# Two chained transformer blocks on one core: experts in pairs, attention by scaling and transposes, log decays in blocks of 16, no identity products

## The chip, the core and the metric

The kernel runs on one core of a Trainium2 chip (trn2), as one launch. The metric is the device time of that core in microseconds (us). TensorE (PE) multiplies, VectorE (DVE), ScalarE (ACT) and GpSimd (POOL) work on the elements, SyncE (SP) issues most of the transfers. [...]

## What is computed

Everything is fp32: 256 tokens of 1024 channels through a first block (twice: sparse attention A, latent attention B, a convolved FFN) and a second block. Cut to what the change touches:

```python
# first block, per layer: two attentions of 8 heads, 2 blocks of 128 queries
p = jax.nn.softmax(logits, axis=-1)                      # per head and block
y = jnp.einsum('bhts,bshd->bthd', p, v)
# second block, gated delta rule: on the context, then on the latent, both directions, chunks of 64
g = -jnp.exp(a_log) * jax.nn.softplus(a + dt_bias)
gc = jnp.cumsum(g.reshape(..., n, CHUNK), axis=-1)       # log decays, 4 chunks of 64
decay = jnp.where(incl, jnp.exp(gc[..., :, None] - gc[..., None, :]), 0.0)
# ... triangular solve per chunk, then a scan over the chunks; beside it RWKV-7:
s = s * w_t[..., None, :] + sa[..., :, None] * b_t[..., None, :] + v_t[..., :, None] * k_t[..., None, :]
# 32 experts in 4 groups, top-1 group and top-2 experts in it
hid = jax.nn.silu(einsum('td,edf->tef', t, w_gate[grp])) * einsum('td,edf->tef', t, w_up[grp])
out = out + jnp.einsum('tef,efd->td', hid * combine[:, grp, :, None], w_down[grp])
```

## The kernel before

Activations lie with channels on the partitions, [128, 8, 256]. Weights come in pieces of 512 KB (SyncE, `wload`), are split into a rounded high half (ScalarE, L452) and the rest (VectorE, L454), and each product is three (L460 to L462, `mm3`). PSUM banks come from `mm` (L421) in turn. The order of the instructions on each engine is set by the framework's scheduler from its own timeline, not by the order of the source, unless a block says otherwise.

By the span of the profile: attention of layer one to about 250 us, FFN and the context's delta rule to 600, attention of layer two 650 to 870, FFN and the context's RWKV to 1220, the latent's projections and delta rule to 1434, its RWKV (preparation to about 1540, then the steps over the chunks) to 1625, outputs to 1680, router, experts 1696 to 1962, last norm.

*Attention* (`attend`, L863). For 4 pairs of heads and 2 query blocks the logits go through the softmax: `pr` is the exponential (L886), `rs` the reciprocal of its row sum (L889). GpSimd multiplies the identity by each column of `rs` (`dg`, L892), TensorE multiplies `pr` by that diagonal (L896), which transposes and scales at once, with one bank per head; VectorE (block 0, L899) or ScalarE (block 1, L901) copies to `pt`, which is multiplied by `v` (L906).

*Log decays* (`gdn_core`, L1182; called once for the context, once for the latent). After softplus (lines to L1246) the prefix sums of 4 chunks are made token by token by 63 dependent adds of 64x4 (L1248); `zb`, `ez` and `tot` are made of them.

*Identity products* (L424). `mm` issues one product of the identity with itself into each new bank whose caller passes one of the names in `HEAT`: in the latent's triangular solves, in the RWKV's preparation, steps and outputs. Nothing reads them. `HEAT` is set in the streams of the latent's part only.

*Experts* (`moe`, L1776). Each expert has 64 slots. `gather` takes the rows of four experts' slots by one-hot products (L1861, L1873, L1880). In each of 16 steps two experts share the array's columns: `up` (L1903), then `down`: silu (L1910 to L1914), two transposes (L1917), copy to `mhT` (L1919), products (L1925), split; `scatter` (L1935) adds to four banks of sums. The weights come in 192 pieces of 512 KB, six for an expert, in two rings of 12 (`AHEAD`, L21) that take turns (`piece`, L2022, L2027); the first ring's are fetched before the experts begin. The source puts step i's `up` ahead of step i-1's `down` and scatter (`finish`), and the scheduler orders the rest.

Of the kernel before, what the change touches and what calls it, by code (L numbers as in the profile page):

```python
# [8 lines left out]
F32 = mybir.dt.float32  # L9
# [45 lines left out]
def col(v):  # L55
    """[..., n*128] -> [128, prod] channel-major columns."""
# [26 lines left out]
def t5_buckets():  # L83
    """bucket of rel = key - query, as t5_bucket has it, for rel in -255..255 (integers only)."""
# [48 lines left out]
def first_layer(i, l):  # L133
    """vectors, weight pieces and the small w_idx weights of one layer of the first block."""
# [48 lines left out]
def bias_tiles(rel_bias):  # L183
    """[128, 8*128 | 8*256]: bias of (query, head, key) for the two blocks of queries."""
# [14 lines left out]
def second_pieces(i):  # L199
# [15 lines left out]
    dn = np.asarray(i["moe_w_down_2"][0], F).reshape(32, 256, D)  # L215
    ps["moe"] = []
    for e in range(32):
        ps["moe"] += pieces(np.concatenate([g[e], u[e]], 1)) + pieces_wide(dn[e])
# [3 lines left out]
SECOND = ("in", "ada", "oa", "ob", "out", "moe")  # L222
# [44 lines left out]
def consts2(c):  # L267
# [4 lines left out]
    for d, tri in enumerate((up, lo)):  # L272
        # row j, column i: j before i (or with it) in the order of the direction, inside a chunk of 64
# [24 lines left out]
def layout(i):  # L298
    """the inputs as the program reads them, and where the parts lie"""
# [14 lines left out]
    for k in SECOND:  # L314
# [4 lines left out]
              "LORA": lora(i), "ROUTER": router(i)}  # L319
    return {k: np.ascontiguousarray(a) for k, a in arrays.items()}, c.at, v.at, woff, w2off  # L320


class Stream:
    """pool of data, scratch and PSUM banks of one strand of the work"""
# [6 lines left out]
class Tagged:  # L331
    """a pool whose tiles take the place of others by name"""
# [16 lines left out]
class Builder:  # L349
    def __init__(self, ctx, tc, I, at_c, at_v):  # L350
# [16 lines left out]
        # the other constants come between the first weights  # L367
# [11 lines left out]
    def phase(self, name, banks=0, t2=0, side="left", pb=1):  # L379
        """a pool that lives as long as a part of the work; with banks and t2 it has PSUM banks and scratch of its own"""  # L380
# [28 lines left out]
    def columns(self, name):  # L409
        """split columns of a layer's input, in place of the last ones"""  # L410
# [16 lines left out]
    def t2(self, name, dt=F32):  # L427
        """scratch of [128, 512]"""
# [6 lines left out]
    def wload(self, src, n=2):  # L435
        """split halves [128, 512] of a piece"""
# [13 lines left out]
    def split(self, hi, lo, x, scale=1.0):  # L450
        """hi + lo = scale * x, hi rounded to what one pass of the tensor engine carries"""
# [32 lines left out]
    def chunk_tok(self, srcs, kt, x, evac):  # L484
        """out[tokens, 512 cols]; evac(b, psum) per 128 tokens."""
# [12 lines left out]
    def rsqrt(self, y, a, t=None):  # L498
        """y = a ** -0.5 for positive a: an integer estimate, a step of third order and one of second"""
# [13 lines left out]
    def rsq(self, ps, rows, inv_n, eps=EPS):  # L513
        """(sums * inv_n + eps) ** -0.5 of sums [rows, 256 tokens] in PSUM, as [128, 2, rows] by token"""
# [11 lines left out]
    def to_rows(self, y, r0, n):  # L526
        """[128, 2, n] by token -> [n, 256]"""
# [7 lines left out]
    def rstd(self, x, kt, r):  # L535
        """r [128, 256] = rstd of the columns of x [128, kt, 256], on every partition"""
# [12 lines left out]
    def rstd_by_token(self, x, kt, cold=False):  # L549
        """[128, 2]: rstd of the columns of x [128, kt, 256], tokens on partitions; cold spares the tensor engine products"""  # L550
# [22 lines left out]
    def scaled(self, x, kt, gain, out):  # L573
        """split of x * gain"""
# [5 lines left out]
    def norm(self, x, kt, gain, out, shift=None, r=None):  # L580
        """rms norm over channels of x [128, kt, 256]: x * rstd * gain (+ shift), split."""
# [13 lines left out]
class First(Builder):  # L595
    """first block"""
# [4 lines left out]
    def mix(self, x, l, filler=None, ahead=None, after=None):  # L601
# [26 lines left out]
        # w_idx, tokens on partitions  # L628
# [39 lines left out]
        class Sums:  # L668
            """sums of squares of 8 query and 8 key heads, a few channels at a time"""
# [11 lines left out]
            def rstd(me, n, scale, name):  # L681
                """rstd * scale of 8 query heads [128, 2, 8] by token; rows() is rstd of 8 key heads [8, 256]"""
# [29 lines left out]
        # keys: rotated shared part  # L712
# [32 lines left out]
        # ---- branch A: rstd of queries and keys by token and head, keys normalized  # L745
# [32 lines left out]
        # ---- gates and merge  # L778
# [27 lines left out]
    def merge_a(self, gate, ya, wa):  # L806
        """gate = (1 + gate) * (ya @ wa)"""
# [6 lines left out]
    def merge_b(self, ga, gate, yb, mg, wb, together=False):  # L814
        """mg = split of (ga + (1 + gate) * (yb @ wb)) / 2"""
# [38 lines left out]
            # 0 for chosen keys, -1e30 for others, added to the bias of each head  # L854
# [8 lines left out]
    def attend(self, rq, v, logits, sels, yh, yl):  # L863
        """normalized, transposed probabilities and their products with v: y^T split, [128, 4, 256]"""
        V, S, G, T = self.V, self.S, self.G, self.T
        for t in range(4):
            # keys on partitions: [keys 0..127 x 256 queries | keys 128..255 x queries 128..255] per head
            pt = self.tmp([128, 2, 384], "pt", bufs=1)
            for b in range(2):
# [20 lines left out]
                dg = self.tmp([128, 2, 128], "dg", bufs=1)  # L890
                for p in range(2):
                    G.tensor_scalar(dg[:, p, :], self.ident, rs[:, p:p + 1], None, op0=ALU.mult)  # L892
                for p in range(2):
                    pp = self.mm()
                    for kk in range(b + 1):
                        T.matmul(pp[:, 128 * kk:128 * kk + 128], pr[:, p, 128 * kk:128 * kk + 128], dg[:, p, :],  # L896
                                 start=True, stop=True)
# [14 lines left out]
    def ffn(self, x, l, filler=None, r=None):  # L912
        """stops once before its first products; without r the norm comes after those"""
# [67 lines left out]
PIT = 4160  # pitch of the triangles of 64 in DRAM: the blocks of 16 on their diagonals lie 1040 apart  # L981
# [3 lines left out]
class Second(First):  # L985
    """second block"""
# [1232 lines left out]
```

## Time and profile before

| | |
|---|---|
| median of 3 runs | 1979.51 us (1979.09 to 1981.39) |
| span of the profiled execution, which is its own time here | 1980.6 us |
| mean granted clock of TensorE | 0.967 |
| busy: TensorE, its weight loads, VectorE, ScalarE, GpSimd | 94%, 79%, 63%, 44%, 17% |
| transfers | 341 MB, mean 172 GB/s |

The span is from the first to the last instruction. A matmul's row shows when its columns enter until its result is out; matmuls overlap, so the pace is read from the starts, not from the lengths. A group's idle time is what its engine stood before it, with what released it.

### The profile page before, as it was taken

How to read it: one execution, taken by the hardware profiler on the slowest of the kernel's cores; microseconds unless marked ns; L12 is line 12 of the kernel's file. 1: busy time of each engine (PE TensorE's matmuls, PEld its weight loads, DVE VectorE, ACT ScalarE, POOL GpSimd, SP SyncE). 2: the span in 40 equal slices, each digit the busy share in tenths (PEclk: the TensorE clock that was granted, in tenths of full speed). 3: DMA queues.
4: the chain of work that ended last, by engine and by line, in shares of the span. 5: the costliest groups of instructions: out<-in, count | busy, mean ns of one | idle time of the engine just before them, and what ended most of it. 6: DMA issues, size and time to landing. Idle time of an engine off the chain costs nothing. (4 is left out here: it accounts for less than half of the span.)

```text
span 1980.6 us, 38175 instructions
## 1 busy us (share of the span) xinstructions
PE 1860.3 (94%) x14934; PEld 1562.4 (79%) x14934; DVE 1242.6 (63%) x2742; ACT 879.5 (44%) x1728; POOL 337.2 (17%) x595
## 2 busy tenths in 40 slices
PE   8999999899999999999999998998998898999996
PEld 7868899698899878898898998888787788545453
DVE  7675578788676785568677766985474376322223
ACT  5555556565445555454445545564232133211111
POOL 0013101315010001205406300034126100000000
PEclk9999999899999999998999999999998899999998
DMA  7454355767645544363533553538003265799981
GB/s 251 143 181 156 111 160 170 270 204 230 183 124 184 154 155 139 88 209 110 145 118 99 150 166 123 160 119 206 27 12 44 37 235 201 298 385 364 390 331 65
DMA packets 169368, 341.43 MB, mean 172 GB/s; under 512 B 89400, under 2 KB 90048, under 8 KB 168288
## 3 DMA queue, kind: packets, MB, share of 16 engines
q1 hardware_dynamic: 160784, 308.75, 48.5%
q0 software_dynamic: 8400, 30.21, 4.1%
q8 instruction: 118, 1.93, 0.4%
q14 instruction: 66, 0.54, 0.1%
HBM read 325.87 MB, written 13.03 MB: 171 GB/s over the span
## 5 line engine op out<-in xcount | busy, mean ns | idle before, releaser
L454 DVE TENSOR_TENSOR wlo<-raw,whi 128x512 fp32r<-128x512 f32 x676 | 476.0, 714 | 234.5 <-ACT whi L452 212.5
L452 ACT ACTIVATE whi<-raw 128x512 fp32r<-128x512 f32 x676 | 421.3, 630 | 437.5 <-PE mm L461 272.7
L460 PE MATMUL mm<-hf,whi 128*128 128x256 f32 x672 | 192.5, 292 | 4.3 <-ACT whi L452 4.3
L461 PE MATMUL mm<-hf,whi 128*128 128x256 f32 x672 | 191.6, 289 | 2.5 <-DVE hf L454 2.5
L462 PE MATMUL mm<-hf,wlo 128*128 128x256 f32 x672 | 185.9, 292 | 4.9 <-DVE wlo L454 4.8
L460 PEld LDWEIGHTS mm<-hf,whi 128*128 128x128 f32 x672 | 129.7, 193 | 11.0 <-ACT whi L452 4.9
L461 PEld LDWEIGHTS mm<-hf,whi 128*128 128x128 f32 x672 | 129.5, 193 | 5.8 <-DVE hf L454 3.7
L462 PEld LDWEIGHTS mm<-hf,wlo 128*128 128x128 f32 x672 | 125.6, 193 | 9.5 <-DVE wlo L454 7.0
L460 PE MATMUL mm<-h,whi 128*128 128x256 f32 x448 | 130.7, 294 | 0.0
L461 PE MATMUL mm<-h,whi 128*128 128x256 f32 x448 | 128.9, 289 | 0.0
L462 PE MATMUL mm<-h,wlo 128*128 128x256 f32 x448 | 128.7, 291 | 0.0
L1903 PE MATMUL mm<-wm,xg 128*64 128x512 f32 x512 | 124.4, 597 | 0.0
L460 PE MATMUL mm<-hl,whi 128*128 128x256 f32 x384 | 111.1, 293 | 9.3 <-ACT hl L452 6.6
L462 PE MATMUL mm<-hl,wlo 128*128 128x256 f32 x384 | 109.7, 294 | 6.0 <-DVE wlo L454 5.8
L461 PE MATMUL mm<-hl,whi 128*128 128x256 f32 x384 | 111.7, 293 | 0.0
L461 PE MATMUL acc<-fl,whi 128*128 128x256 f32 x352 | 99.2, 286 | 0.0
L460 PE MATMUL acc<-fh,whi 128*128 128x256 f32 x352 | 98.7, 286 | 0.0
L462 PE MATMUL acc<-fh,wlo 128*128 128x256 f32 x352 | 96.2, 285 | 0.0
L1903 PEld LDWEIGHTS mm<-wm,xg 128*64 128x64 f32 x512 | 36.9, 137 | 66.6 <-issue 60.8
L460 PEld LDWEIGHTS mm<-h,whi 128*128 128x128 f32 x448 | 85.0, 190 | 4.6 <-issue 3.5
L461 PEld LDWEIGHTS mm<-h,whi 128*128 128x128 f32 x448 | 85.2, 190 | 3.7 <-issue 3.6
L892 POOL TENSOR_SCALAR dg<-cblob,rs 128x128 f32<-128x128 f32 x64 | 44.7, 708 | 253.3 <-DVE rs L889 213.3
(696 smaller groups left out, 4717.9 us busy)
## 6 DMA issues: line engine op xcount, KB each, us to landing
raw<-in_W_dram SPq DMA_DIRECT2D x336, 512.0 KB, 3.7
wm<-in_W_dram SPq DMA_DIRECT2D x192, 512.0 KB, 8.1
wada<-in_W_dram POOLq DMA_DIRECT2D x48, 512.0 KB, 6.5
lora<-in_LORA_dram SPq DMA_DIRECT2D x2, 1280.0 KB, 6.8
bm<-in_BIAS_dram SPq DMA_DIRECT2D x2, 1024.0 KB, 4.9
tri_ef<-tge SPq DMA_DIRECT2D x4, 512.0 KB, 8.2
gates<-gate SPq DMA_DIRECT2D x8, 256.0 KB, 4.5
mgate<-gates SPq DMA_DIRECT2D x2, 1024.0 KB, 5.1
```

The costliest lines, as they stand in the source:

```text
L452: self.S.activation(hi, x, AF.Copy, scale=scale)
L454: self.V.tensor_tensor(lo, x, hi, op=ALU.subtract)
L460: self.T.matmul(out, wh, xh, start=first, stop=False, **k)
L461: self.T.matmul(out, wh, xl, start=False, stop=False, **k)
L462: self.T.matmul(out, wl, xh, start=False, stop=last, **k)
L892: G.tensor_scalar(dg[:, p, :], self.ident, rs[:, p:p + 1], None, op0=ALU.mult)
L1903: T.matmul(gu[64 * p:64 * p + 64, :], xe[:, k, 128 * j + 64 * p:128 * j + 64 * p + 64], ws[p][k // 2][:, 512 * (k % 2):512 * (k % 2) + 512 ...
```

## The change

Four edits. The lines of the changed kernel are shifted (L424 is gone, L460 is L463, L896 is L898, L1606 to L1694 are L1615 to L1703, L1861 is L1870, L1903 is L1912, L1917 is L1930, L1925 is L1942, L1935 is L1952).

```diff
-AHEAD = (12, 12)
-HEAT = {'prep': 1, 'tri': 1, 'steps': 1, 'out': 1}
+AHEAD = (6, 7)
+HEAT = {}
...
-    for e in range(32):
-        ps['moe'] += pieces(np.concatenate([g[e], u[e]], 1)) + pieces_wide(dn[e])
+    for e in range(0, 32, 2):
+        both = [pieces(np.concatenate([g[p], u[p]], 1)) + pieces_wide(dn[p]) for p in (e, e + 1)]
+        ps['moe'] += [np.concatenate(ab, 1) for ab in zip(*both)]
...
+    arrays['WM'] = np.stack(ps['moe'])
...
-                dg = self.tmp([128, 2, 128], 'dg', bufs=1)
+                V.tensor_tensor(pr[:, :, :nk], pr[:, :, :nk], rs[:, :, None].to_broadcast([128, 2, nk]), op=ALU.mult)
+                pp = self.mm()
                 for p in range(2):
-                    G.tensor_scalar(dg[:, p, :], self.ident, rs[:, p:p + 1], None, op0=ALU.mult)
-                for p in range(2):
-                    pp = self.mm()
                     for kk in range(b + 1):
-                        T.matmul(pp[:, 128 * kk:128 * kk + 128], pr[:, p, 128 * kk:128 * kk + 128], dg[:, p, :], start=True, stop=True)
-                    if b == 0:
-                        V.tensor_copy(pt[:, p, 0:128], pp[:, :128])
-                    else:
-                        S.activation(pt[:, p, 128:384], pp[:, :256], AF.Copy)
+                        o = nk * p + 128 * kk
+                        T.transpose(pp[:, o:o + 128], pr[:, p, 128 * kk:128 * kk + 128], self.ident)
+                src = pp[:, :2 * nk].rearrange('p (a k) -> p a k', a=2)
+                if b == 0:
+                    V.tensor_copy(pt[:, :, 0:128], src)
+                else:
+                    S.activation(pt[:, :, 128:384], src, AF.Copy)
...
-        x3 = x.rearrange('p (c i) -> p c i', c=4)
-        for i in range(1, 64):
-            V.tensor_tensor(x3[:, :, i:i + 1], x3[:, :, i:i + 1], x3[:, :, i - 1:i], op=ALU.add)
+        one = self.tmp([64, 256], 'gone', bufs=1)
+        V.memset(one, 1.0)
+        V.memset(one[:, 0:256:16], 0.0)
+        V.tensor_copy(t[0:32], x[0:32])
+        V.tensor_copy(t[32:64], rev(x[32:64], 256))
+        V.tensor_tensor_scan(z1, one, t, 0.0, ALU.mult, ALU.add)
+        bl = self.tmp([64, 3, 16], 'gbl', bufs=1)
...
+        V.tensor_tensor_scan(bl[:, 2], bl[:, 0], bl[:, 1], 0.0, ALU.mult, ALU.add)
+        z16 = lambda y: y.rearrange('p (b i) -> p b i', b=16)
+        V.tensor_tensor(z16(z2), z16(z1), bl[:, 2, :, None].to_broadcast([64, 16, 16]), op=ALU.add)
...
-        def down(gu, cs, j, ws):
+        def act_cols(gu, cs, j):
...
+        def act_rows(th):
...
+        def down(hT, ws):
...
-        for i in range(16):
-            if i % 2 == 0:
-                xe, oht, cs = rows(2 * i)
-            ws = ahead()
-            gu = up(xe, i % 2, ws)
-            if queue:
-                finish()
-            queue.append((i, oht, gu, cs, i % 2, ws))
-        finish()
+        with self.tc.manual_schedule(engines={mybir.EngineType.PE}):
+            nxt = rows(0)
+            th, hT, ys = (None, None, [])
+            for i in range(18):
+                if i < 16:
+                    if i % 2 == 0:
+                        xe, oht, cs = nxt
+                    ws = ahead()
+                    gu = up(xe, i % 2, ws)
+                if 0 < i < 17:
+                    hT = act_rows(th)
+                if i < 16:
+                    th = act_cols(gu, cs, i % 2)
+                if i > 1:
+                    scatter(acc, *ys.pop(0), i % 2, i == 2, i == 17)
+                if 0 < i < 17:
+                    ys.append((down(hT, wd), od))
+                if i < 16:
+                    wd, od = (ws, oht)
+                if i % 2 and i < 15:
+                    nxt = rows(2 * i + 2)
...
-        t = self.wm[i % sum(AHEAD) >= AHEAD[0]].tile([128, 1024], F32, name='wm')
-        self.nc.sync.dma_start(t, self.I['W2'][self.w2off['moe'] + i // 12 * 12 + i % 2 * 6 + i % 12 // 2])
+        t = self.wm[i % sum(AHEAD) >= AHEAD[0]].tile([128, 2, 1024], F32, name='wm')
+        self.nc.sync.dma_start(flat(t), self.I['WM'][i])
```

The weights of two experts lie side by side in a tensor of their own, 96 pieces of 1 MB; the rings hold 6 and 7 of them. `down` is cut in three: `act_cols` (silu), `act_rows` (transposes and copy) and `down` (products and split). `ws[p][k]` becomes `ws[k][:, p]` in both products. The prefix sums run in token order for one half of the partitions and against it for the other: a scan within blocks of 16 tokens, one over the sums of the blocks of a chunk, and one add.

On TensorE the scheduler's order of a period of the experts was this (`up` is L1903 on `wm` and `xg`, the scatter L1935 on `oht` and `my`, the gather L1861, L1873, L1880; the number at the end is how many instructions stand in a row):

```order
8692 L1903 MATMUL mm<-wm,xg 64x512 x16
8693 L1917 MATMUL mm<-cblob,mth 128x128 x2
8694 L1925 MATMUL mm<-wm,mhT 64x512 x8
8695 L1903 MATMUL mm<-wm,xg 64x512 x9
8696 L1935 MATMUL acc_19863<-oht,my 128x256
8697 L1935 MATMUL acc_19864<-oht,my 128x256
8698 L1903 MATMUL mm<-wm,xg 64x512
8699 L1935 MATMUL acc_19863<-oht,my 128x256 x3
8700 L1935 MATMUL acc_19864<-oht,my 128x256 x3
8701 L1935 MATMUL acc_19865<-oht,my 128x256 x4
8702 L1935 MATMUL acc_19866<-oht,my 128x256 x4
8703 L1903 MATMUL mm<-wm,xg 64x512 x6
```

In the changed kernel two steps stand written out by hand (`up` L1912, transposes L1930, scatter L1952, `down` L1942):

```order
8554 L1912 MATMUL mm<-wm,xg 64x512 x16
8555 L1930 MATMUL mm<-cblob,mth 128x128 x2
8556 L1952 MATMUL acc_19505<-oht,my 128x256 x4
8557 L1952 MATMUL acc_19506<-oht,my 128x256 x4
8558 L1952 MATMUL acc_19507<-oht,my 128x256 x4
8559 L1952 MATMUL acc_19508<-oht,my 128x256 x4
8560 L1942 MATMUL mm<-wm,mhT 64x512 x8
8561 L1912 MATMUL mm<-wm,xg 64x512 x16
8562 L1930 MATMUL mm<-cblob,mth 128x128 x2
8563 L1952 MATMUL acc_19505<-oht,my 128x256 x4
8564 L1952 MATMUL acc_19506<-oht,my 128x256 x4
8565 L1952 MATMUL acc_19507<-oht,my 128x256 x4
```

No product of `up` or of the gather is cut any more, the scatter stands between the transposes and the `down` that needs their copy, and it is that of the step before.

In the RWKV's preparation TensorE's order before was this (`rtw`, `rsig`, `rAR`, `rbig` are the preparation's operands; L424 is the identity product):

```order
8109 L424 MATMUL mm<-cblob 128x128 x2
8110 L1606 MATMUL mm<-lora,rtw 128x128 x4
8111 L424 MATMUL mm<-cblob 128x128 x3
8112 L1606 MATMUL mm<-lora,rtw 128x128 x4
8113 L1667 MATMUL mm<-rAR,rbig 128x128 x16
8114 L424 MATMUL mm<-cblob 128x128 x2
8115 L1620 MATMUL mm<-cblob,rsig 128x256 x8
8116 L424 MATMUL mm<-cblob 128x128
8117 L1678 MATMUL mm<-cblob,rbig 128x128 x4
8118 L424 MATMUL mm<-cblob 128x128
8119 L1678 MATMUL mm<-cblob,rbig 128x128 x4
8120 L424 MATMUL mm<-cblob 128x128
```

And in the changed kernel, with the same operands and no L424:

```order
8064 L1615 MATMUL mm<-lora,rtw 128x128 x4
8065 L1629 MATMUL mm<-cblob,rsig 128x256 x4
8066 L1615 MATMUL mm<-lora,rtw 128x128 x4
8067 L1676 MATMUL mm<-rAR,rbig 128x128 x16
8068 L1629 MATMUL mm<-cblob,rsig 128x256 x4
8069 L1642 MATMUL mm<-lo,cblob 128x256
8070 L1648 MATMUL mm<-lo,lora 128x256 x2
8071 L1687 MATMUL mm<-cblob,rbig 128x128 x8
8072 L1692 MATMUL mm<-cblob,rxv 64x128 x4
```

The products on which the preparation waits now stand next to each other, with the scheduler's own choice of which comes first.

## Rows read from the trace of the kernel before

**Rows 1.** The page, busy time of each engine, share of the span, instructions.

```profile
PE 1860.3 (94%) x14934; PEld 1562.4 (79%) x14934; DVE 1242.6 (63%) x2742; ACT 879.5 (44%) x1728; POOL 337.2 (17%) x595
```

**Rows 2.** Timeline of PE, experts: start, length (us), engine, line, operation, records, [idle].

```profile
1721.58 7.09 PE L1903 MATMUL mm<-wm,xg 128*64 128x512 f32 x32
1728.60 0.44 PE L1917 MATMUL mm<-cblob,mth 128*128 128x128 f32 x2
1729.55 3.65 PE L1925 MATMUL mm<-wm,mhT 128*64 128x512 f32 x16 [0.52 <-DVE mhT L1919]
...
1733.03 4.45 PE L1903 MATMUL mm<-wm,xg 128*64 128x512 f32 x18
...
1738.86 1.93 PE L1935 MATMUL acc<-oht,my 128*128 128x256 f32 x14
1740.71 2.79 PE L1903 MATMUL mm<-wm,xg 128*64 128x512 f32 x12
...
1751.87 2.08 PE L1861 MATMUL mm<-oh,ht 128*128 128x256 f32 x16
1753.78 0.95 PE L1873 MATMUL mm<-comb,oh 128*128 128x2 f32 x8
...
1755.16 2.37 PE L1903 MATMUL mm<-wm,xg 128*64 128x512 f32 x10
```

**Rows 3.** Stretches of the experts (busy by engine, PEclk, DMA share, GB/s), and a wait.

```profile
1730.00:1740.00 10.00, 10.00 (x47) 3.93 (x44) 1.78 (x3) 1.19 (x2) 0.00 (x0) 1.00 1.03 420
1700.00:1900.00 200.00, 193.71 (x1050) 95.61 (x1048) 48.08 (x106) 38.34 (x79) 0.00 (x0) 1.00 0.97 379
PEld mm L1903 <- DMA wm<-in_W_dram: 1.9, 7, 0.3
```

**Rows 4.** Groups by line, whole span: records, busy us, mean ns, idle before.

```profile
L892 POOL TENSOR_SCALAR dg<-cblob,rs 128x128 f32<-128x128 f32 x64 | 44.7, 708 | 253.3 <-DVE rs L889 213.3 <-PE mm L461 24.5 <-PE mm L1052 7.3
L896 PE MATMUL mm<-dg,pr 128*128 128x128 f32 x192 | 32.4, 283 | 1.6 <-POOL dg L892 1.5
L1669 DVE TENSOR_TENSOR rGA<-mm,cblob 128x256 f32<-128x256 f32 x32 | 12.7, 407 | 0.2
```

**Rows 5.** A stretch of the first layer's attention, all engines.

```profile
150.00:200.00 50.00, 50.00 (x364) 40.76 (x363) 24.61 (x58) 28.73 (x76) 15.43 (x23) 1.00 0.48 155
```

**Rows 6.** Groups by line: log decays on VectorE, whole span.

```profile
L1248 DVE TENSOR_TENSOR grow<-grow 64x4 f32<-64x4 f32 x126 | 21.1, 168 | 1.5
L1241 DVE SCALAR_TENSOR_TENSOR grow<-grow 64x256 f32<-64x256 f32 x12 | 4.9, 409 | 0.0
```

**Rows 7.** The two stretches of the log decays, all engines.

```profile
384.00:450.00 66.00, 66.00 (x554) 63.25 (x553) 58.41 (x167) 43.70 (x79) 6.22 (x15) 0.97 0.61 196
1262.00:1316.00 54.00, 54.00 (x401) 49.36 (x401) 46.54 (x145) 33.26 (x62) 2.41 (x3) 0.95 0.45 138
```

**Rows 8.** Stretches of the last recurrence, instructions of L424 alone (PE, PEld).

```profile
1434.00:1490.00 56.00, 15.39 (x83) 12.14 (x84) 1.00 0.07 13
1490.00:1540.00 50.00, 14.11 (x56) 9.77 (x54) 0.79 0.29 41
1553.00:1592.00 39.00, 8.56 (x40) 5.72 (x40) 0.99 0.16 50
1500.00:1512.00 12.00, 3.73 (x11) 2.89 (x12) 0.50 0.31 48
```

**Rows 9.** Stretches of the last recurrence, all engines.

```profile
1440.00:1490.00 50.00, 47.18 (x425) 40.63 (x424) 39.53 (x113) 20.15 (x43) 13.67 (x21) 1.00 0.08 14
1490.00:1540.00 50.00, 39.67 (x457) 34.56 (x457) 19.03 (x40) 8.51 (x15) 33.97 (x75) 0.79 0.29 41
1553.00:1592.00 39.00, 38.95 (x530) 33.45 (x526) 19.08 (x41) 6.94 (x20) 5.40 (x4) 0.99 0.16 50
```

**Rows 10.** Timeline of PE: transposes of the preparation, then products of the attention.

```profile
1508.51 1.06 PE L1678 MATMUL mm<-cblob,rbig 128*128 128x128 f32 x4
...
141.28 1.06 PE L896 MATMUL mm<-dg,pr 128*128 128x128 f32 x8
```

More of the change, by code (lines that the diff above doesn't have):

```diff
@@ L216, in second_pieces @@
     ps["moe"] = []
-    for e in range(32):
-        ps["moe"] += pieces(np.concatenate([g[e], u[e]], 1)) + pieces_wide(dn[e])
+    for e in range(0, 32, 2):
+        both = [pieces(np.concatenate([g[p], u[p]], 1)) + pieces_wide(dn[p]) for p in (e, e + 1)]
+        ps["moe"] += [np.concatenate(ab, 1) for ab in zip(*both)]
     return ps
-SECOND = ("in", "ada", "oa", "ob", "out", "moe")
+SECOND = ("in", "ada", "oa", "ob", "out")
 def lora(i):
@@ L319, in layout @@
               "LORA": lora(i), "ROUTER": router(i)}
+    arrays["WM"] = np.stack(ps["moe"])
     return {k: np.ascontiguousarray(a) for k, a in arrays.items()}, c.at, v.at, woff, w2off
@@ L1244, in gdn_core @@
         V.tensor_scalar(x, x, na, None, op0=ALU.mult)
-        x3 = x.rearrange("p (c i) -> p c i", c=4)
-        for i in range(1, 64):
-            V.tensor_tensor(x3[:, :, i:i + 1], x3[:, :, i:i + 1], x3[:, :, i - 1:i], op=ALU.add)
+        rev = lambda t, n: bass.AP(t.tensor, t.offset + n - 1, [[t.ap[0][0], 32], [-1, n]])
+        one = self.tmp([64, 256], "gone", bufs=1)
+        V.memset(one, 1.0)
+        V.memset(one[:, 0:256:16], 0.0)
+        V.tensor_copy(t[0:32], x[0:32])
+        V.tensor_copy(t[32:64], rev(x[32:64], 256))
@@ new lines, in gdn_core @@
+        V.tensor_tensor_scan(z1, one, t, 0.0, ALU.mult, ALU.add)
+        bl = self.tmp([64, 3, 16], "gbl", bufs=1)
+        V.memset(bl, 0.0)
+        V.memset(bl[:, 0], 1.0)
+        V.memset(bl[:, 0, 0:16:4], 0.0)
+        V.tensor_copy(bl[:, 1].rearrange("p (c b) -> p c b", c=4)[:, :, 1:], z1.rearrange("p (c b i) -> p c b i", c=4, b=4)[:, :, :3, 15])
+        V.tensor_tensor_scan(bl[:, 2], bl[:, 0], bl[:, 1], 0.0, ALU.mult, ALU.add)
+        z16 = lambda y: y.rearrange("p (b i) -> p b i", b=16)
@@ L1257, in gdn_core @@
+        V.tensor_copy(zb[32:64], rev(z2[32:64], 256))
         S.activation(zb[64:128], ab[64:128], AF.Tanh, scale=0.5)
         V.tensor_scalar(zb[64:128], zb[64:128], 0.5, 0.5, op0=ALU.mult, op1=ALU.add)
[L1259 to L1264 removed]
@@ L1265, in gdn_core @@
-        V.tensor_scalar(e1[32:64], zb3[32:64], -1.0, None, op0=ALU.mult)
+        tot = self.tmp([64, 4], "gtot", bufs=1)
+        zb3 = zb.rearrange("p (c i) -> p c i", c=4)
+        V.tensor_copy(tot[0:32], zb3[0:32, :, 63])
+        V.tensor_copy(tot[32:64], zb3[32:64, :, 0])
+        V.tensor_copy(ez[:, 0], zb[:64])
+        V.tensor_tensor(ez[:, 1].rearrange("p (c i) -> p c i", c=4), tot[:, :, None].to_broadcast([64, 4, 64]), zb3[:64], op=ALU.subtract)
         S.activation(flat(ez), flat(ez), AF.Exp)
@@ L1882, in gather, with weights @@
             return xe, oht, cs
-        def weights(src):
+        def weights(i):
             out = []
             for j in range(6):
-                t = self.wm[1].tile([128, 1024], F32, name="wm")
-                nc.sync.dma_start(t, src[j])
+                t = self.wm[1].tile([128, 2, 1024], F32, name="wm")
+                nc.sync.dma_start(flat(t), self.I["WM"][bass.ds(6 * i + j, 1)].rearrange("o p c -> (o p) c"))
                 out.append(t)
@@ L1892, in ahead @@
         def ahead():
-            while len(self.queue) < 12:
+            while len(self.queue) < 6:
                 self.piece()
-            ws, self.queue = [self.queue[p:12:2] for p in range(2)], self.queue[12:]
+            ws, self.queue = self.queue[:6], self.queue[6:]
             return ws
@@ L1914, in down @@
             V.tensor_tensor(th, th, u, op=ALU.mult)
+            return th
+        def act_rows(th):
             pt = self.mm()
@@ L1919, in down @@
             V.tensor_copy(flat(hT), pt[:, :256])
+            return hT
+        def down(hT, ws):
             y = tmp.tile([128, 2, 1024], F32R, name="my")
@@ L1936, in scatter @@
                              stop=last and s == 1, skip_group_check=True)
-        base = self.w2off["moe"]
         rows = lambda e: gather(pos[:, :, e:e + 4], comb[:, :, e:e + 4], 4, (act, own)[e // 4 % 2])
-        queue = []
-        def finish():
-            i, oht, *a = queue.pop()
-            scatter(acc, down(*a), oht, i % 2, i == 0, i == 15)
-        for i in range(16):
-            if i % 2 == 0:
-                xe, oht, cs = rows(2 * i)
-            ws = ahead()
-            gu = up(xe, i % 2, ws)
-            if queue:
-                finish()
-            queue.append((i, oht, gu, cs, i % 2, ws))
-        finish()
+        with self.tc.manual_schedule(engines={mybir.EngineType.PE}):
+            nxt = rows(0)
+            th, hT, ys = None, None, []
+            for i in range(18):
[13 more added lines that the diff above has]
+                if i < 16:
+                    wd, od = ws, oht
+                if i % 2 and i < 15:
+                    nxt = rows(2 * i + 2)
         add = lambda k, part: V.scalar_tensor_tensor(x[:, k, :], part[k // 2][:, 256 * (k % 2):256 * (k % 2) + 256], m[:, 40 + k, 0:1],
@@ L1966, in moe @@
                 with self.tc.For_i(0, 16, 1) as i:
-                    src = lambda p: [self.I["W2"][bass.ds(base + 12 * i + 6 * p + j, 1)].rearrange("o p c -> (o p) c") for j in range(6)]
                     xe, oht, cs = gather(V2[:, 0, :, 0:2], V2[:, 1, :, 0:2], 2, act)
-                    ws = [weights(src(p)) for p in range(2)]
-                    y = down(up(xe, 0, ws), cs, 0, ws)
+                    ws = weights(i)
+                    y = down(act_rows(act_cols(up(xe, 0, ws), cs, 0)), ws)
                     a = [accp.tile([128, 512], F32, name=f"acc{q}", tag=f"acc{q}", bufs=1) for q in range(4)]
@@ L2025, in piece @@
         self.pieces += 1
-        t = self.wm[i % sum(AHEAD) >= AHEAD[0]].tile([128, 1024], F32, name="wm")
-        self.nc.sync.dma_start(t, self.I["W2"][self.w2off["moe"] + i // 12 * 12 + i % 2 * 6 + i % 12 // 2])
+        t = self.wm[i % sum(AHEAD) >= AHEAD[0]].tile([128, 2, 1024], F32, name="wm")
+        self.nc.sync.dma_start(flat(t), self.I["WM"][i])
         self.queue.append(t)
```

21 lines of the change are left out of this document (4 added, 17 removed).

## The prediction

> **What bounds the kernel now.** First the page's busy times: TensorE is busy 94% of the span, no other engine is near it [rows 1]. So a microsecond is won only where TensorE stops issuing something, stops waiting, or runs at the higher of its two clocks. Then the stages. In the experts (1696 to 1962 us) the sequence of TensorE is regular: one period holds two steps of two experts each and lasts 1755.16 - 1721.58 = 33.58 us [rows 2], so eight periods make the stage. The reader is to see three things in [rows 2]: the 32 records of `up` take 7.02 us when nothing is put between them (1721.58 to 1728.60); the odd step's `up`, cut by the scatter into pieces of 18, 2 and 12 records (two to a product of the order above), spreads from 1733.03 to 1743.5; and behind the two transposes TensorE stands 0.52 us until VectorE has copied them to `mhT`. The transfers are the second bound there: 379 GB/s over 200 us, 420 in the densest 10 us, and TensorE waited for a weight in all 1.9 us [rows 3].
>
> In the attention TensorE is full (50.00 of 50 us) while VectorE has 24.61 [rows 5]; the second layer's is alike. In the two stretches of the log decays VectorE is the full one: 58.41 of 66 and 46.54 of 54 us, TensorE full beside it [rows 7]. [...]
>
> **The experts: -17 us.** Removed: the cuts and the wait; the work is the same. A period of the new order, all from [rows 2]: two `up` at 7.02 = 14.04; two `down` at 3.48 (1729.55 to 1733.03) = 6.96; two scatters, 14 records in 1.85 us (1738.86 to 1740.71), so 16 in 2.1, together 4.2; two pairs of transposes at 0.44, 0.9; the gather's 32 products at the 1.91 us that 16 take (1751.87 to 1753.78), 3.82; and its 12 small ones 1.38 (1753.78 to 1755.16). Sum 31.3, 2.3 under 33.58. The wait for `mhT` goes because the scatter of 2.1 us now stands between transposes and `down`; the copy took TensorE's 0.52. Late next: the gather no longer has scatter pieces between its products, so its banks must be emptied at the pace at which TensorE fills them, which I count at 0.2 per period. 2.1 by 8 is 17; bounds 0 (the transfers, first rival) and 20 (2.5 by 8). SyncE issues 96 transfers of 1 MB for 192 of half that; a weight's buffer comes free as before, when the last product on it is done. A period moves 24 old pieces, 12.58 MB: in 31.3 us that is 402 GB/s, above the 379 of the mean and below the 420 of the densest stretch. I take it as covered, because the 379 hold pauses in which the ring was full, and TensorE waited so little.
>
> [...]
>
> **The attention: -9 us.** 96 fp32 products with the scaled diagonal are 192 records; eight of them take 1.06 us, four transposes the same in a stretch at the lower clock (granted 0.50) [rows 4, 8, 10], and a 128x128 transpose leaves one record each (two for the two of [rows 2]). So 96 records of 0.12 us go, 11.5 us. GpSimd loses 44.7 us of work, for which TensorE waited 1.6 us in all [rows 4]. VectorE gets 32 multiplies: 16 of 128x256 at 0.41 us (the nearest row is L1669, [rows 4]), 16 of 128x512 at no more than twice that, 20 us in all, and loses half of the copies' launches. They stand on the chain from softmax to product, but with VectorE idle half the time and other projections to issue I count them at 2.5 us. Bounds -11.5 and 0.
>
> **The log decays: -4 us.** 126 dependent adds, 21.1 us, 10.5 per call, become about 17 instructions, most on 64x256, where the nearest row (L1241) has 0.41 us [rows 6]; the scan itself appears in no row: at least that 0.41, at most the adds it replaces. I take 0.8 for the two scans of a call, near the row, and 4 us a call for all. VectorE gains 6 us in each stretch. In 384 to 450 TensorE issues 554 records in 66 us, 0.119 each, the pace of full feed: nothing is won. In 1262 to 1316 it issues 401 in 54 us, 0.135 each; at 0.119 that would be 47.7, 6 less [rows 7]. I take 4; bounds 0 and -6.
>
> **The identity products: -6 us.** 114 of them go. In 1553 to 1592 they cover 8.56 us of a full TensorE [rows 8, 9]; I take 6, since the steps' chain through VectorE and ScalarE stays. In 1434 to 1490 they cover 15.39 us, but VectorE sets the pace: 2. In 1490 to 1540 they cover 14.11 us that GpSimd and VectorE leave empty; taking them away wins nothing, and the clock may stay low longer: +2. Bounds -15 and, short of the third rival, +8.
>
> **Sum:** -17 - 9 - 4 - 6 = -36 against the profiled execution's 1980.6 us: 1944.6; the median of the runs is 1.1 lower, so **1943.5 us**. The scheduler orders all else anew, which I count at nothing, give or take 6. A difference of 0.2% (4 us) is about what a measurement can tell from none.
>
> **Rivals.** *First, the transfers become the bound of the experts.* For: 402 GB/s would be wanted, 379 was the mean, 97% of the queues' time. Against: the 420, and 1.9 us of waits [rows 3]. At 379 a period lasts 33.2 us, 0.4 less than now: 3 us instead of 17 won, 1957 us. Chance 0.12.
>
> *Second, only the experts' part shows.* TensorE in the attention, the decays and the recurrence would wait as long for the softmax, the weights' halves and the steps as it now works on what is removed. For: VectorE gets 20 us more in the attention, and it is as full as TensorE in the decays [rows 7]. Against: TensorE's 50.00 of 50 [rows 5]. 1980.6 - 17 - 1.1, 1962 us. Chance 0.18, 0.02 of it so reduced that no difference shows.
>
> *Third, slower: without the identity products the clock falls.* From 1434 to 1553 they cover some 30 us of TensorE's time, and 1490 to 1540 is already at 0.79 with them. [...] Against: from 1553 TensorE is full without help. Chance 0.10, 0.02 of it within 0.2%. [...]
>
> That the change does not do what it says is excluded for the order on TensorE, which stands above; for the single scan instruction it is not, and that costs at most the 4 us of the decays.
>
> **Numbers.** Forecast 0.60, the rivals 0.12, 0.18 and 0.10. Faster by over 0.2%: 0.60 + 0.12 + 0.16 = 0.88; within 0.2%: 0.04; slower: 0.08. The range: down to all bounds together, -20 - 11.5 - 6 - 15 = -52.5, near 1927, and 5 more for the order; up to the second rival and the scheduler's 6 with it, 1969. The third rival is left out: 1922 to 1970.
>
> **What would show it.** Experts right: the period near 31.3 us, no wait for `mhT`, all `up` in one piece of 7.0; wrong: waits of TensorE for `wm`, a transfer share near 1 throughout. Attention right: 0 to 250 us shorter by some 4, 650 to 870 the same; wrong: waits for `pr` from VectorE. Decays right: the scan under 1 us, and the stretch behind 1262 shorter. Products right: 1434 to 1625 shorter by 6 with a granted clock no lower; wrong: a granted clock under 0.8 in 1440 to 1490 or 1540 to 1590, and that stretch longer than its 191 us. A time over 1981 us would make the forecast wrong, and the clock of that stretch would be the first thing to look at.

## The result and the profile after

The changed kernel takes 1935.22 us (median of 4 runs, 1933.0 to 1938.79) where the kernel before takes 1980.45 (4 runs): a ratio of 0.9768, 95% interval 0.975 to 0.9787, by which it is 46 us faster. The forecast was 1943.5 us, 36 faster. The profiled execution, that of 1938.79, has a span of 1937.0 us, 43.6 less than that of before. The page's busy times, as in [rows 1], and TensorE's clock in 40 slices of the span (in tenths; a clock is given here as the granted share of full speed, at every moment of both traces 0.50 or 1.00):

```profile
PE 1797.9 (93%) x14610; PEld 1522.1 (79%) x14610; DVE 1240.7 (64%) x2650; ACT 876.2 (45%) x1712; POOL 290.1 (15%) x531
PEclk9989999899999998999899999899997798899998
```

TensorE lost 62 us of busy time and 324 records, and is about as full as before (93%, then 94%); the mean clock fell from 0.967 to 0.953.

Two steps of the experts in the timeline of TensorE (start, length, engine, line, operation, records), to be laid beside [rows 2]:

```profile
1700.04 7.09 PE L1912 MATMUL mm<-wm,xg 128*64 128x512 f32 x32
1707.06 0.44 PE L1930 MATMUL mm<-cblob,mth 128*128 128x128 f32 x2
1707.26 2.12 PE L1952 MATMUL acc<-oht,my 128*128 128x256 f32 x16
1709.31 3.65 PE L1942 MATMUL mm<-wm,mhT 128*64 128x512 f32 x16
1712.79 7.04 PE L1912 MATMUL mm<-wm,xg 128*64 128x512 f32 x32
...
1725.61 4.08 PE L1870 MATMUL mm<-oh,ht 128*128 128x256 f32 x32
1729.54 0.95 PE L1882 MATMUL mm<-comb,oh 128*128 128x2 f32 x8
...
1730.91 1.51 PE L1912 MATMUL mm<-wm,xg 128*64 128x512 f32 x6
```

`up` is whole (7.02 us, 1700.04 to 1707.06), the scatter fills the time in which `mhT` is copied, and no wait stands in brackets, as an idle time of TensorE would. The period is 1730.91 - 1700.04 = 30.87 us, where the forecast had 31.3 and before 33.58. TensorE is never idle in 200 us, while the transfers run at 391 GB/s (as in [rows 3]):

```profile
1700.00:1900.00 200.00, 200.00 (x1134) 102.22 (x1134) 51.18 (x111) 40.83 (x83) 0.00 (x0) 1.00 0.95 391
```

The stage of the experts, from the first `up` to the last scatter, went from 266.0 us (1695.87 to 1961.85) to 243.8 (1676.26 to 1920.05).

The parts of the attention by line, as in [rows 4] (records, busy us, mean ns, idle before):

```profile
L898 PE MATMUL mm<-cblob,pr 128*128 128x128 f32 x96 | 15.9, 277 | 1.1 <-DVE pr L893 1.1
L893 DVE TENSOR_TENSOR pr<-pr,rs 128x512 f32<-128x512 f32 x16 | 11.0, 686 | 0.3
L893 DVE TENSOR_TENSOR pr<-pr,rs 128x256 f32<-128x256 f32 x16 | 6.7, 421 | 0.4
L901 DVE COPY pt<-mm 128x256 f32<-128x256 f32 x16 | 6.7, 419 | 5.0 <-PE mm L898 4.9
```

96 records in place of 192, 17.7 us of multiplies on VectorE, 2.4 less of copies, and TensorE waited 1.1 us for them all.

The first two stretches of the last recurrence, as in [rows 9]:

```profile
1434.00:1490.00 56.00, 43.35 (x381) 36.70 (x380) 49.62 (x126) 18.23 (x38) 21.38 (x38) 0.84 0.07 13
1490.00:1540.00 50.00, 32.66 (x553) 30.44 (x554) 9.61 (x21) 8.95 (x16) 24.24 (x58) 0.73 0.45 67
```

The clock there did fall, to 0.84 and 0.73, from 1.00 and 0.79. And yet the stretch from the RWKV's first preparation product to its last step became 16 us shorter. That is what the experiments had to explain.

Where the 43.6 us lie, from the starts of the same instructions in the two traces: to the first product of the RWKV's preparation 7.9 us (it starts at 1434.8, now at 1426.9); from there to the last product of the steps, which the text below calls the recurrence, 16.5 (it lasted 186.6, now 170.1); from there to the first `up` 4.8 lost (74.5, now 79.3); the experts 22.2; the end 1.8.

### The profile page after: what moved, and what is told of

Same layout as the page of the kernel before. It is cut to its first block, busy times and chain, and to the rows that moved or that the text cites. A ratio compares the mean times of both kernels' runs of the same rounds, so it can differ in the third digit from the quotient of the medians.

```text
span 1937.0 us, 37106 instructions
## 1 busy us (share of the span) xinstructions
PE 1797.9 (93%) x14610; PEld 1522.1 (79%) x14610; DVE 1240.7 (64%) x2650; ACT 876.2 (45%) x1712; POOL 290.1 (15%) x531
## 5 line engine op out<-in xcount | busy, mean ns | idle before, releaser
L463 PE MATMUL mm<-hf,whi 128*128 128x256 f32 x672 | 194.0, 293 | 1.3 <-ACT whi L455 1.3
L463 PEld LDWEIGHTS mm<-hf,whi 128*128 128x128 f32 x672 | 130.2, 194 | 8.8 <-ACT u L952 2.6
L463 PE MATMUL mm<-h,whi 128*128 128x256 f32 x448 | 130.8, 293 | 0.0
L463 PE MATMUL mm<-hl,whi 128*128 128x256 f32 x384 | 111.3, 294 | 10.9 <-ACT hl L455 6.6
L1912 PE MATMUL mm<-wm,xg 128*64 128x512 f32 x512 | 112.8, 594 | 0.0
L463 PE MATMUL acc<-fh,whi 128*128 128x256 f32 x352 | 98.5, 285 | 1.0 <-DVE u L954 1.0
L1912 PEld LDWEIGHTS mm<-wm,xg 128*64 128x64 f32 x512 | 36.1, 137 | 69.9 <-issue 64.7
L463 PEld LDWEIGHTS mm<-h,whi 128*128 128x128 f32 x448 | 84.7, 189 | 2.8 <-issue 2.6
L465 PEld LDWEIGHTS mm<-h,wlo 128*128 128x128 f32 x448 | 84.4, 189 | 2.3 <-issue 1.3
```

Of the source, the lines that this page charges most:

```text
L463: self.T.matmul(out, wh, xh, start=first, stop=False, **k)
L465: self.T.matmul(out, wl, xh, start=False, stop=last, **k)
L1912: T.matmul(gu[64 * p:64 * p + 64, :], xe[:, k, 128 * j + 64 * p:128 * j + 64 * p + 64], ws[k // 2][:, p, 512 * (k % 2):512 * (k % 2) + 512 ...
```

## The experiments

Each kernel was timed against the kernel before on its own chip; the ratios are to that, and a difference in us is the ratio's, on the scale of the first figures. Traces are of one execution each. Eight kernels, the changed one among them, issue the same products in the same order on TensorE up to 353 us, and their traces stand 5.6 to 9.8 us ahead of the kernel before there: a lead of a few us between two traces can be that of one execution. First the parts alone, each put into the kernel before.

**The experts alone.**

```diff
-AHEAD = (12, 12)
+AHEAD = (6, 7)
...
+        with self.tc.manual_schedule(engines={mybir.EngineType.PE}):
```

(and the rest of the hunks on `moe`, `piece`, `WM`)

> The kernel before with the experts' part of the change alone (pieces of two experts, order by hand). Theory A (each part is worth the TensorE time that it takes out of its own stage, and the parts add): the two traces show the experts' stage go from 266.0 to 243.8 us, so this kernel is 22 us faster than before, near 1958, with a period of 30.9 us and nothing moved ahead of 1676. Rival B (the stage is faster only because it starts in a better state, or the scheduler moves other stages with it): under 15 or over 29 us.

Measured: ratio 0.9891 (0.9873 to 0.9909), 21.6 us faster. The period is 30.87 us and the stage 243.8 us, both as in the changed kernel. Theory A holds: this part is worth what it takes out of its own stage. (At the first `up` its trace is 4.2 us ahead already, no more than single traces differ by.)

**The attention alone.**

```diff
-                    G.tensor_scalar(dg[:, p, :], self.ident, rs[:, p:p + 1], None, op0=ALU.mult)
...
+                V.tensor_tensor(pr[:, :, :nk], pr[:, :, :nk], rs[:, :, None].to_broadcast([128, 2, nk]), op=ALU.mult)
...
+                        T.transpose(pp[:, o:o + 128], pr[:, p, 128 * kk:128 * kk + 128], self.ident)
```

> The kernel before with the attention's part alone. Theory A: both attentions end earlier by what the slots of 96 records give, 5 to 6 us each, and it stays: 11 us faster, near 1969. Rival B (what is won in the attention is given back in the stages behind, as the changed kernel's lead falls from 11 us at 890 to some 3 at 1220): 2 to 5 us faster, near 1976, with the lead at 890 still at 11.

Measured: 0.9948 (0.9929 to 0.9967), 10 us faster. The last products with `pt` of A's attention in the trace, by line (one row for a kernel: before, this one, the changed one; length in ns, first and last start):

```profile
L907 PE MATMUL mm<-pt,va x32: 272/273/273, 175.3 to 855.0; 128*64 128x128 f32 x32
```

```profile
L906 PE MATMUL mm<-pt,va x32: 272/272/273, 170.7 to 836.5; 128*64 128x128 f32 x32
```

```profile
L909 PE MATMUL mm<-pt,va x32: 272/273/273, 175.2 to 843.0; 128*64 128x128 f32 x32
```

With the part alone the second layer's attention ends 18.5 us earlier, in the changed kernel 12.0, so more than the slots of the 96 records (11.5). Of the 6.5 us between the two, 3.0 stand at 353 us already, up to which both issue the same products, so they are not the other parts' doing. Alone, 8 us are given back in the recurrence, which lasts 194.7 us there. What remains, 10 us, is near theory A's 11.

**The log decays alone.**

```diff
-        for i in range(1, 64):
-            V.tensor_tensor(x3[:, :, i:i + 1], x3[:, :, i:i + 1], x3[:, :, i - 1:i], op=ALU.add)
...
+        V.tensor_tensor_scan(z1, one, t, 0.0, ALU.mult, ALU.add)
```

> The kernel before with the log decays' part alone. Theory A: nothing at 600, 5 us earlier at 1320, and 4 to 5 us faster in all, near 1976. Rival B (the tri behind it waits for something else, or the new order costs as much): within 2 us of before.

Measured: 1.002 (1.0004 to 1.0035), 4 us slower. Rival B, and past it. The scan itself is short, as the group in the changed kernel shows:

```profile
L1254 DVE TENSOR_TENSOR_SCAN grow<-gone,grow 64x256 f32<-64x256 f32 x2 | 1.3, 674 | 0.0
```

0.67 us where the forecast had taken 0.8 for both scans of a call. VectorE does get its time back (from 1220 to 1410 it is busy 129.4 us where it was 136.6), and in the latent's call TensorE does go faster: from the last product of the latent's norms (L1198, 1286.6 before) to the last of its gram products (L1317, 1325.2 before) the seven kernels with the new decays in that call take 29.8 to 35.0 us, the seven with the old ones 38.7 to 43.3; this one takes 34.3. It is lost again behind: the first product of the RWKV's preparation starts at 1445.0, 10.2 us later than before, and the granted clock from 1220 to 1410 is 0.92 where it was 0.96.

**No identity products, alone.**

```diff
-HEAT = {'prep': 1, 'tri': 1, 'steps': 1, 'out': 1}
+HEAT = {}
```

> The kernel before without identity products. Theory A (they cost TensorE's time): the stretch 1434 to 1625 shorter by 10 to 17 us with a granted clock of 0.85 to 0.9 there, and 10 to 12 us faster in all, near 1969. Rival B (the clock they kept up is worth what they cost; the changed kernel's gain there comes from the decays or the scheduler): within 4 us of before, and granted clock under 0.87 there.

Measured: 0.9944 (0.9924 to 0.9963), 11 us faster. But not where theory A put it: in the trace the recurrence lasts 186.0 us (1421.3 to 1607.3) where it lasted 186.6, at a clock of 0.84 where it was 0.93. Either the slots saved and the clock lost cancel there, or neither counts; this run does not tell which. The gain lies ahead of it, where the scheduler lets the preparation begin 13.5 us earlier.

The four parts alone give 21.6 + 10 - 4 + 11 = 39 us, together 46; with 3 to 4 us of uncertainty on each figure these 7 us are not clear of noise. But the recurrence of 170.1 us is in none of the four traces: it lasts 186.8, 194.7, 182.9 and 186.0 us there, and that arises only where the parts meet. The next four divide the experts, and undo parts of the changed kernel.

**TensorE's order of the experts by hand, the transfers as before.**

```diff
-        finish()
...
+        with self.tc.manual_schedule(engines={mybir.EngineType.PE}):
```

(and the rest of the hunks on `moe`; 192 pieces of 512 KB and `AHEAD = (12, 12)` stay)

> The kernel before with TensorE's order of the experts written by hand and its 192 transfers of 512 KB in rings of 12 and 12 left as they were. Theory A (the order gives the gain, by the cuts and the wait that it removes): the period is 30.9 us as with pairs, the kernel 20 to 22 us faster than before. Rival B (at 512 KB the transfers could not feed that period): period 31.5 to 33 us with waits of TensorE for wm, 5 to 14 us faster.

Measured: 0.9881 (0.9855 to 0.9906), 23.6 us faster, period 30.87 us, stage 243.85. Theory A: the order gives it all. Over 200 us of the stage:

```profile
1700.00:1900.00 200.00, 199.39 (x1123) 100.88 (x1122) 51.47 (x113) 40.39 (x83) 0.00 (x0) 1.00 1.01 403
```

The small pieces feed that period too, at 403 GB/s and a share of 1.01; the changed kernel's 1 MB pieces needed 0.95 for 391.

**Pairs of 1 MB, the scheduler's order.**

```diff
-AHEAD = (12, 12)
+AHEAD = (6, 7)
...
-    for e in range(32):
+    for e in range(0, 32, 2):
```

> The kernel before with pairs of 1 MB in rings of 6 and 7, the scheduler ordering TensorE. Theory A: the period stays at 33 to 34 us and the time within 4 us of before, since TensorE hardly waited for a weight. Rival B (half of the gain is the transfers'): period under 32.5 us, 8 us or more faster.

Measured: 0.9932 (0.9905 to 0.9959), 13.5 us faster: rival B by the time, but not by its cause. The periods are 33.59, 32.98, 31.79, 31.51, 33.31 and 32.74 us. The first of 33.59 has the order of before, row for row, cuts and wait with it; in the shorter ones the scheduler put the odd step's transposes ahead of the scatter. It found part of the order that was then written by hand.

**The changed kernel with the old decays.**

```diff
-        V.tensor_tensor_scan(z1, one, t, 0.0, ALU.mult, ALU.add)
...
+        for i in range(1, 64):
+            V.tensor_tensor(x3[:, :, i:i + 1], x3[:, :, i:i + 1], x3[:, :, i - 1:i], op=ALU.add)
```

> The changed kernel with the log decays token by token again, 63 adds a call. Theory A (the decays' part wins nothing on TensorE and costs some us of half clock behind it, as alone): 2 to 5 us faster than the changed kernel, near 1932 where before has 1981. Rival B (with the other parts it does win its 5 us, seen at 1320): 4 to 6 us slower than the changed kernel, near 1940.

Measured: 0.9738 (0.9717 to 0.9759). On the scale of the first figures that is 1929 us (1924 to 1933), 6 us under the changed kernel with intervals that overlap: theory A's sign, and not clear of noise. Its trace is another one, though: the preparation begins 17 us earlier (1409.7) and the recurrence lasts 189.2 us where the changed kernel's lasts 170.1.

**The changed kernel with products in the preparation.**

```diff
-HEAT = {}
+HEAT = {'prep': 1}
```

> The changed kernel with the identity products back in the RWKV's preparation alone, none in solves, steps and outputs. Theory A (they cost TensorE's time only where it is full, and in the preparation they held the clock): granted clock of 1434 to 1540 back from about 0.8 to over 0.88, and 4 to 10 us faster than the changed kernel. Rival B (VectorE and GpSimd set the pace of the preparation at either clock): within 3 us of the changed kernel, or slower by what the products take.

Measured: 0.9844 (0.9827 to 0.986), some 15 us slower than the changed kernel: rival B by its sign. The recurrence lasts 191.8 us, 22 more; 56 products at 0.4 us would be as much (in [rows 8] 83 records, two to a product, take 15.39 us), but the kernel with old decays, which has none, is nearly as long.

**With products in solves and steps.**

```diff
-HEAT = {}
+HEAT = {'tri': 1, 'steps': 1}
```

> The changed kernel with the identity products back in the solves and the steps (54 of the 114), none in preparation and outputs. The products in the preparation alone cost 20 us, all 114 together 11 (taken from the kernel before). Theory A (so those of the solves and steps win some 7 to 9 back, by the clock): 5 to 9 us faster than the changed kernel, granted clock of 1490 to 1540 back from 0.73 to over 0.85. Rival B (they cost TensorE's time as well, 0.4 us each between small products, and the 11 against 20 is the scheduler's order): 0 to 15 us slower than the changed kernel.

(52 products: the 114 less 56 and 6.) Measured: 0.9908 (0.9876 to 0.994), 28 us slower than the changed kernel, more than either theory has; the recurrence lasts 193.8 us and the clock in it is 0.83.

So the traces of the recurrence fall into two kinds: it lasts 170 to 174 us in the changed kernel and the three runs below, 183 to 195 us in the other ten. What divides them is seen in where one product of the preparation stands, the last one (L1694 before); the RWKV's four pairs of heads are taken two by two. Stretches from the first preparation product to the first solve, from there to the last step, counting that line's records alone. Before, without products, and the changed kernel with old decays, with products in the preparation:

```profile
1434.80:1516.10 81.30, 4.57 (x64) 4.02 (x64) 0.92 0.16 26
1516.10:1621.40 105.30, 5.57 (x64) 4.75 (x64) 0.94 0.34 87
```

```profile
1421.30:1501.10 79.80, 5.34 (x64) 4.84 (x64) 0.83 0.15 22
1501.10:1607.30 106.20, 6.51 (x64) 6.34 (x64) 0.86 0.32 84
```

```profile
1409.70:1484.60 74.90, 4.52 (x64) 4.07 (x64) 0.86 0.16 24
1484.60:1598.90 114.30, 6.73 (x64) 6.31 (x64) 0.87 0.33 87
```

```profile
1424.50:1504.20 79.70, 4.57 (x64) 4.02 (x64) 0.87 0.15 22
1504.20:1616.30 112.10, 4.31 (x64) 3.95 (x64) 0.86 0.34 88
```

And the changed kernel:

```profile
1426.90:1510.20 83.30, 8.50 (x128) 7.82 (x128) 0.83 0.19 29
1510.20:1597.00 86.80, 0.00 (x0) 0.00 (x0) 0.90 0.35 93
```

In the first four, 64 of the 128 records, those of the second two pairs of heads, come behind the first solve. In the changed kernel all 128 come ahead of it, and it takes hardly longer to get there: 83 us against 75 to 81. The rest then takes 87 us instead of 105 to 114. In its first stretch TensorE waits for VectorE (in total, times, longest):

```profile
PE mm L1676 <- DVE rbig L1656: 7.3, 3, 3.9
PE mm L1629 <- DVE rsig L1618: 2.0, 2, 1.1
```

The waits for `rbig` were 1.4 us before. So TensorE has room there (43.35 of 56 us busy from 1434 to 1490), and the preparation goes by at VectorE's pace (49.62 of 56). The product L1694 is a mark of the order, not itself the cause: the solve reads the other half of `rGA`. What the second two pairs' solve does wait for is its back substitution on GpSimd and the DMA that brings the result. The substitution's first instruction and the first product that waited for its result, before and in the changed kernel:

```profile
1524.06 0.22 POOL L1099 TENSOR_TENSOR tri_p<-tri_d,tri_e 128x15 f32<-128x15 f32 x1 [6.58 <-DVE tri_d L1096]
1549.20 0.27 PE L1129 MATMUL mm<-tri_ef,tri_x 64*64 64x64 f32 x1 [3.01 <-DMA tri_ef<-tr1e]
```

```profile
1505.61 0.22 POOL L1101 TENSOR_TENSOR tri_p<-tri_d,tri_e 128x15 f32<-128x15 f32 x1 [4.91 <-DVE tri_d L1098]
1526.52 0.33 PE L1131 MATMUL mm<-tri_ef,tri_x 64*64 64x64 f32 x2 [1.88 <-DMA tri_ef<-tr1e]
```

Counted from the first product of the preparation that is 89.3 and 114.4 us before, 78.7 and 99.6 in the changed kernel: 14.8 of the 16.5 us are won by then. The substitution starts after 86 to 94 us in the ten long traces and after 78 to 79 in the four short ones. One caution: in the kernel with old decays the preparation's first product is 17 us earlier and its recurrence ends at 1598.9, 1.9 us behind the changed kernel's, so the length alone overstates what the order is worth there. That the order makes the difference is read from fourteen traces; no kernel set it by hand.

**Products in the outputs alone.**

```diff
-HEAT = {}
+HEAT = {'out': 1}
```

> The changed kernel with the identity products back in the outputs alone, 6 or so of them. Theory A (the lead of the recurrence falls from 25 us at 1608 to 20 at 1625 because the clock falls there): granted clock of 1600 to 1680 higher, 2 to 5 us faster than the changed kernel. Rival B (too few to hold the clock): within 2 us.

Measured: 0.972 (0.9689 to 0.9751), which touches the changed kernel's interval. From the last step to the first `up`, all engines, the changed kernel and this one:

```profile
1597.00:1676.26 79.26, 67.73 (x492) 61.94 (x490) 50.20 (x155) 28.98 (x54) 2.59 (x2) 0.87 0.60 228
```

```profile
1591.30:1666.70 75.40, 66.31 (x509) 61.14 (x507) 50.00 (x155) 28.84 (x54) 2.58 (x2) 0.91 0.63 240
```

75.4 us at 0.91 against 79.3 at 0.87, and 74.5 at 0.91 before: theory A's figures for this stretch. Its cause is not shown: the next kernel takes 75.4 us there at 0.93 and the one with old decays 74.8 at 0.84, and neither has these products. Of the 9.6 us that this trace is ahead of the changed kernel's at the first `up`, 6.0 stand before the preparation begins.

**22 products in the steps, TensorE's order otherwise kept.**

```diff
-HEAT = {}
+HEAT = {'steps': 1}
```

> The changed kernel with 22 identity products back, those of the steps. TensorE's order is otherwise that of the changed kernel, all preparation ahead of the solves, so what the products themselves cost stands alone. Theory A (slots, 0.3 to 0.4 us each where TensorE is full): solves and steps 5 to 9 us longer, 5 to 9 us slower than the changed kernel. Rival B (the order is what counts; the products fall into the steps' waits): 170 us from the first rtw product to the last of the steps as in the changed kernel, and within 3 us of its time.

Measured: 0.9758 (0.9743 to 0.9773), against 0.9768 of the changed kernel: the same. All 128 records are ahead of the solves, and the recurrence lasts 173.7 us (1426.7 to 1600.4), 3.6 more. Rival B is the nearer: a product costs 0.16 us there (3.6 by 22), not 0.4, while the same order is kept.

**Old decays in the context's call alone.**

```diff
-                self.gdn_core(ctx["X"], ab, False, tg)
+                self.gdn_core_old(ctx["X"], ab, False, tg)
```

(`gdn_core_old` is the routine of before)

> The changed kernel with the token by token decays in the context's call alone, the blocks of 16 in the latent's. TensorE's order keeps all preparation ahead of the solves. Theory A (the new decays in the context win nothing, and with them the stages to 1290 lost the lead of the attention; the order of the preparation gives the rest): some 10 us ahead of the changed kernel at 1290, 170 us from rtw to the last of the steps, near 1925, which would beat both kernels. Rival B (that lead in the kernel with old decays in both calls was one run's clock): within 4 us of the changed kernel.

Measured: 0.969 (0.9673 to 0.9707), 1924 us beside 1984.5 of before: faster than both kernels, than the changed one by some 15 us. The recurrence lasts 169.9 us, all 128 records ahead. The same product of the latent's norm starts at 1290.1 us before, at 1283.4 in the changed kernel and at 1268.2 here: leads of 6.7 and 21.9 us. Of these 15.2 us, 3.6 stand at 353 us already, up to which the two issue the same products. Then the place of the context's delta rule differs. Its solves by line, in the changed kernel and here (516.8 to 523.9 before):

```profile
L1142 PE MATMUL mm<-tri_x,tri_ef x64: 218/218/219, 464.3 to 471.1; 64*64 64x64 f32 x64
```

```profile
L1142 PE MATMUL mm<-tri_x,tri_ef x64: 218/218/218, 506.4 to 513.4; 64*64 64x64 f32 x64
```

With the new decays these solves came 52 us earlier, a lead that no later stage shows, and the stretch from 870 to 1220 behind was poorer, at a lower clock and with fewer records (0.96 and 3055 with the old ones):

```profile
870.00:1220.00 350.00, 331.16 (x2981) 307.59 (x2980) 255.55 (x515) 171.04 (x319) 106.26 (x214) 0.94 0.46 131
```

From the end of the second layer's attention (last product of its projection, 871.4 before) to the end of the FFN (1207.7), the five kernels that have both the new attention and the new decays in the context take 342 to 343 us, the nine others 335 to 339. So the loss there goes with these two edits together; why TensorE's order is the poorer for it is not shown, since no kernel held the rest of the order fixed.

## Why the prediction was right, and where its steps were not

*The experts* (-17, measured -22.2 in the trace, -21.6 alone). The mechanism was right, point by point: cuts gone, wait gone, transfers fast enough for a TensorE that is busy 200.00 of 200 us. Mis-sized was the term of the transposes, 0.44 a pair: TensorE goes on 0.20 us after their start (1707.06 to 1707.26), and the 0.2 per period for the gather's banks did not come. So a full period gained 2.71 us, over the 2.5 of the bound, and the bound of 20 was too low. The sum's eight like periods are seven and a rest: five gained 2.71 each, the first and the last 1.9 and 4.3 (25.71 to 23.78 and 35.15 to 30.87), what follows them 2.4. The first rival fell twice: TensorE full at 391 GB/s, and at 403 with small pieces.

*The attention* (-9, measured -10 alone). The size was right. The lead at its end is larger than the bound (12.0 and 18.5 us); alone, 8 us of it were given back in the recurrence.

*The log decays* (-4, measured +4 alone). Wrong in sign, and the step that failed is not the one with the 6 us. In the latent's call the runs are as forecast or better: the kernel with old decays and the last one differ in that call alone, and the ratios are 0.9738 and 0.969, some 9 us; in the traces 6.4 of them lie between the norms and the gram products (41.4 and 35.0 us). What failed is "In 384 to 450 TensorE issues 554 records in 66 us, 0.119 each, the pace of full feed: nothing is won". Nothing was won, but what follows behind was counted at nothing too, and with the other parts the new decays cost some 15 us there, the difference of the changed kernel and the last one; about 7 of them lie between 871 and 1207 in the traces. The price of the scan was near: 0.67 us, 1.65 times the 0.409 of [rows 6].

*The identity products* (-6, measured -11 alone and -16.5 in the recurrence of the changed kernel). The sign was right, the mechanism was not. "In 1553 to 1592 they cover 8.56 us of a full TensorE; I take 6" priced slots; 22 of them put back cost 3.6 us in the trace and nothing that the runs tell from none. What the change won in that stretch came with an order in which the second two pairs' preparation, substitution and solve are earlier; the forecast counted the scheduler's order at nothing, "give or take 6". Recurrences with the other order last 16 to 24 us longer than the changed kernel's among those shown above, and the order comes and goes with edits elsewhere: the changed kernel's edits together bring it, none of the four parts alone does, and products in preparation or solves, or old decays in the latent's call, undo it.

*The third rival* half came true: the clock fell as it said, to 0.84 and 0.73. What the lower clock costs that stretch by itself no run shows. TensorE was busy 43.35 of 56 us and 32.66 of 50 there, so it had room, and the recurrence lasted 170.1 us for 186.6.

So the sum was nearer than its terms, and that is luck in part: 22 us won for 17, 4 lost for 4 won in the decays, and the scheduler's order, which was put at zero, came with most of the 16.5 us of the last recurrence and with the loss behind the context's decays.

## What to carry to other kernels

Where a scheduler orders an engine, lay the new order beside the old at every stage that the edit touches and price the order itself: here the recurrence lost 16.5 us with another order of its preparation, while the 114 products taken out alone left its length as it was (186.0 for 186.6). Ask of each stage whether the engine waits in it: in that recurrence TensorE was busy 169.4 us before and 149.7 without the products, and fewer instructions at a lower clock (0.84 for 0.93) together brought no gain and no loss; in the experts, where it is full (200.00 of 200 us), a period gained what the rows say, to 0.4 us (2.71 for 2.3). And try each part of a change alone and also taken out of the whole: the decays cost time in one of their two calls and won it in the other.

## What was not expected of the hardware

Transfers of 1 MB took less of the queues' time than those of half the size: 391 GB/s at a share of 0.95 (412 per full share), 403 at 1.01 (399). The recurrence took 186.0 us at a mean clock of 0.84 without identity products and 186.6 at 0.93 with them, so the products taken out and 9 points of clock lost together left the length as it was. What remains open is why the scheduler puts the second two pairs' preparation ahead only with the new decays in the latent's call, and where the 13.5 us before the recurrence without products come from.
